# Between two layers of a transformer trunk: an overflow branch ahead of the last down projection, eight row fetches issued together, a store on another queue

## The chip, the cores and the metric

The kernel runs on one core of one Trainium2 chip. The metric is the device time of one execution in microseconds (us); the times shown are medians of several executions.

## The reference, cut to what matters

Two layers work on 256 latent tokens and 256 context tokens of width 1024, in float32. Each layer is an attention mixer and then a mixture of 16 experts, of which each token takes two. The second layer (layer 1) has no experts for the context.

```python
for layer in range(DEPTH):                                   # DEPTH = 2
    ...                                                      # norm, w_in, four attention groups, w_out
    x = x + m_lat[5] * moe_ffn(h2, router_w, router_b, w_gate[layer], w_up[layer], w_down[layer])
    if need_ctx:                                             # layer 0 alone
        ctx = ctx + m_ctx[5] * moe_ffn(hc2, ...)

# in moe_ffn, for a block of tokens of expert e
(jax.nn.silu(xe @ w_gate[e]) * (xe @ w_up[e])) @ w_down[e]
y = jnp.zeros_like(hf).at[buf_t].add(yb * buf_w[:, None])    # two rows per token
```

## The kernel before, in words

Weights come as transfers of 1 MB through a ring of slots, all from SyncE's queue (`stream`, `pump`, line 125). `next_w` takes the next one, `done_w` gives its slot back and issues the next load that a free slot allows.

The experts of layer 0 are the class `Moe`. Each expert has room for 96 tokens (CAP). Its tokens are gathered from DRAM, `first` multiplies with gate and up, `hidden` makes the SwiGLU product and transposes it into `hT` (ACT evacuates it, line 1061), and `second` is the down projection. `second` has a main part for 64 tokens (`py`, line 1075) and a rest for the other 32 (`py2`, line 1081); the weights come in two blocks, `hf` 0 and 1, and for each block the main part runs and then the rest. `store` multiplies both with the gates on VectorE (lines 1100 and 1104), and POOL scatters the rows into the DRAM buffer `yd` with one indirect DMA each (line 991). The matrix products are pinned in their program order; all else is placed on the engines' queues by a scheduler at build time, which knows the data's dependencies and a program order as priority.

Where an expert got more than 96 tokens, `overflow` computes the others in a loop inside a conditional block. Each engine reads the counter `mxi` into a register (line 1144) and jumps over the body by itself (line 1145). With the inputs here the body isn't run. Behind a jump not into the body, an engine adjusts the semaphores that the body would have moved: SyncE waits for its DMA lanes, POOL for the lanes of its scatters, and then runs INC_SWDGE_SEM. The call stands behind the last expert.

Then layer 1 begins with `make_hT`. For each tile of 128 tokens (0 and 1 latent, 2 and 3 context) `combine` fetches both rows of each token from `yd` into a buffer `yy` (two DMAs of 512 KB from SyncE's queue, three buffers), adds them to x with the routing weights (VectorE, line 1224) and, for tiles 0 and 1, stores x to DRAM from SyncE's queue (line 1226), for a reload much later. Then ACT squares the tile (line 406), POOL and VectorE make the norm (lines 299, 418), TensorE transposes two tiles at a time (line 429), and the projections of layer 1 begin (line 469; their weights are split in two halves at lines 456 and 458).

Of the kernel before, what the change touches and what calls it, by code (L numbers as in the profile page):

```python
# [11 lines left out]
F32 = mybir.dt.float32  # L12
# [8 lines left out]
D = 1024  # L21
L = 2
# [3 lines left out]
NE = 16  # L26
# [26 lines left out]
def body(tc, a, dbg=None):  # L53
    nc = tc.nc
    ctx = ExitStack()
    V, S, G, PE = nc.vector, nc.scalar, nc.gpsimd, nc.tensor

    def pool(name, bufs=1, space=None, stack=None, side=None):
        kw = {} if space is None else dict(space=space)
        if side is not None:  # L60
            kw["side"] = side
        return (stack or ctx).enter_context(tc.tile_pool(name=name, bufs=bufs, reuse_waits="tile", **kw))
# [9 lines left out]
    def psum(tag):  # L72
        return ps.tile([128, 512], F32, name=tag, bufs=dict(mm=2, ada=1, tr=2, S=2, o=1)[tag])
# [44 lines left out]
    def drop_ring(tag):  # L118
        assert all(x[0] != tag for x in used)
        slots_free[:] = [x for x in slots_free if x[0] != tag]  # L120


    def stream(out, in_):
        with tc.issue_after(state["dma"]) if state["dma"] is not None else nullcontext():
            state["dma"] = nc.sync.dma_start(out, in_).ins

    def pump():
        while slots_free and state["emit"] < len(jobs):
            nm, view, src = jobs[state["emit"]]
            xs = [y for y in slots_free if y[0] == "a" or nm[0] in "eo"]  # L130
            if not xs:
                break
            x = xs[0]
            slots_free.remove(x)
            t = slot(x)
            tv = t.rearrange("p (k n) -> p k n", n=view)
            stream(tv, src.rearrange("(k p) n -> p k n", p=128))
            issued.append((nm, x, tv))
            state["emit"] += 1

    def next_w(nm):
        if not issued:
            pump()
        n, tag, t = issued.pop(0)
        assert n == nm, (n, nm)
        used.append(tag)
        return t


    def done_w(n=1):  # L150
        for _ in range(n):
            slots_free.append(used.pop(0))
        pump()
# [66 lines left out]
    X = {}  # L220
# [559 lines left out]
    x1d = dram.tile([256, D], F32, name="x1d")  # L780

    class Moe:
# [281 lines left out]
        def second(self, e):  # L1064
            l, hT = self.l, self.hT
            py = psum("S")
            py2 = psum("S") if self.CAP > 64 else None
            for hf in range(2):
                wd = next_w(f"e{l}")
                for g in range(2):  # L1070
                    f = 2 * hf + g
                    for c in range(self.tiles_m):
                        m = 128 // self.tiles_m
                        t, h = c % (64 // m), 512 * (m * c // 64)
                        self.order(PE.matmul(py[m * c:m * c + m], lhsT=hT[:, f, m * t:m * t + m], rhs=wd[:, g, h:h + 512],  # L1075
                                             start=f == 0, stop=f == 3))
                if py2 is not None:
                    for g in range(2):
                        f = 2 * hf + g
                        for c in range(4):  # L1080
                            self.order(PE.matmul(py2[32 * c:32 * c + 32, 0:256],
                                                 lhsT=hT[:, 4 + f % 2, 32 * (f // 2):32 * (f // 2) + 32],
                                                 rhs=wd[:, g, 256 * c:256 * c + 256], start=f == 0, stop=f == 3))
                done_w()
            self.store(e, py, py2)


# [19 lines left out]
        def experts(self, p2):  # L1107
            self.p2, self.xt = p2, {}
            self.start()
            self.fetch(0)  # L1110
            p = self.first(0, lambda: self.fetch(1))
            for e in range(NE):
                q = self.next(e, p)
                self.second(e)
                p = q

# [72 lines left out]
        def general(self, ei, xT):  # L1189
            l, p2 = self.l, self.p2  # L1190
            pgs = []
            for nm in ("w_gate", "w_up"):
                pg = psum("mm")
                for k in range(8):
                    wk = p2.tile([128, 1, 512], F32, name="wk", bufs=2)
                    nc.sync.dma_start(wk, a[nm][l, bass.ds(ei, 1), 128 * k:128 * k + 128].rearrange("e p n -> p e n"))
                    PE.matmul(pg, lhsT=xT[:, k], rhs=wk[:, 0], start=k == 0, stop=k == 7)
                pgs.append(pg)
            sg, h = self.wide()
            S.activation(sg, pgs[0], AF.Silu)  # L1200
            V.tensor_mul(h, sg, pgs[1])
            pt = psum("tr").rearrange("p (q n) -> p q n", n=128)
            for k in range(4):
                PE.transpose(pt[:, k], h[:, 128 * k:128 * k + 128], ident)
            hT = p2.tile([128, 4, 128], F32, name="hT", bufs=2)
            S.activation(hT, pt, AF.Copy)
            y = p2.tile([128, D], F32, name="yo")
            for hf in range(2):
                py = psum("S")
                for f in range(4):  # L1210
                    wk = p2.tile([128, 1, 512], F32, name="wk", bufs=2)
                    nc.sync.dma_start(wk, a["w_down"][l, bass.ds(ei, 1), 128 * f:128 * f + 128,
                                                      512 * hf:512 * hf + 512].rearrange("e p n -> p e n"))
                    PE.matmul(py, lhsT=hT[:, f], rhs=wk[:, 0], start=f == 0, stop=f == 3)
                V.tensor_copy(y[:, 512 * hf:512 * hf + 512], py)
            return y


        def combine(self, t, scr):
            yy = scr.tile([128, 2, D], F32, name="yy", bufs=3)  # L1220
            for k in range(2):
                stream(yy[:, k], yd[self.l][256 * t + k:256 * t + 256:2])
            for k in range(2):
                V.scalar_tensor_tensor(X[t], yy[:, k], self.wts[:, t, k:k + 1], X[t], op0=OP.mult, op1=OP.add)
            if t < 2:
                nc.sync.dma_start(x1d[128 * t:128 * t + 128], X[t])


    class MoeOnChip(Moe):
# [232 lines left out]
    for l in range(L):  # L1462
# [8 lines left out]
        hT = [hp.tile([128, 8, 512], F32R, name=f"hT{i}") for i in range(2)]  # L1471
# [31 lines left out]
        g = GROUPS[-1]  # L1503
# [9 lines left out]
        scr = pool(f"op{l}", stack=stR, side=P)  # L1513
# [5 lines left out]
        moe = (Moe if l < L - 1 else MoeOnChip)(l, tiles, pers, scr)  # L1519
# [20 lines left out]
        p2 = pool(f"moe{l}", stack=stM, side=P)  # L1540
        if l < L - 1:

            moe.g5 = {}
            for s in range(len(tiles) // 2):
                g = moe.g5[s] = p2.tile([128, 768], F32, name=f"g5{s}")
# [11 lines left out]
                nc.scalar.dma_start(moe.gate[64 * c:64 * c + 64], amd[r:r + 1].to_broadcast([64, 512]))  # L1557
        with ExitStack() as stE:
            moe.experts(pool(f"moee{l}", stack=stE, side=P))
            if l < L - 1:  # L1560
                moe.overflow()
        drop_ring("c")
        drop_ring("b")
        stB.close()
# [117 lines left out]
```

## Time and profile before

| | us |
|---|---|
| median of three runs | 1228.17 |
| lowest and highest of them | 1224.29, 1228.35 |
| the profiled execution | 1229.28 |
| its span, first to last instruction | 1227.5 |
| TensorE busy in the span | 1119.5 (91%) |
| VectorE, ACT, POOL busy | 568.3, 417.2, 239.9 |

The span is what the trace covers; its zero is the first instruction. Busy counts instructions that an engine executes; jumps, semaphore waits and the issue of a DMA belong to the sequencer in front of the engine and stand under the engine's name with a q. "PEld" is TensorE's weight load, and PEldq the sequencer that serves both. In a timeline the bracket behind a line is the engine's idle time before it, and what ended it.

### The profile page before, as it was taken

The page shows a single profiled execution, that of the slowest core. Times are in us where ns is not written, and L with a number is a line of the kernel's source. Part 1 is how long each engine was busy: PE and PEld are TensorE (multiplying, and loading weights), DVE is VectorE, ACT ScalarE, POOL GpSimd, SP SyncE. Part 2 cuts the span into 40 slices and gives each one's busy share as a digit, 9 for nine tenths or more (in the row PEclk, how much of TensorE's full clock was granted, in tenths as well). Part 3 has the DMA queues.
Part 4 walks back from the last instruction along what each step waited for, and adds up shares of the span by engine and source line. Part 5 has one row for each costly group of instructions (what it writes and reads, how often), then busy time and mean ns, then how long its engine had stood idle before and what let it go on. Part 6 is the DMA issues. An engine that isn't in the chain of part 4 may idle for free. (4 is left out here: it accounts for less than half of the span.)

```text
span 1227.5 us, 21408 instructions
## 1 busy us (share of the span) xinstructions
PE 1119.5 (91%) x8495; PEld 654.6 (53%) x8495; DVE 568.3 (46%) x1545; ACT 417.2 (34%) x1003; POOL 239.9 (20%) x265
## 2 busy tenths in 40 slices
PE   4999999999999949999999992899999979999996
PEld 2677667676645424444444432888887443443432
DVE  4465766556433563232222225976775442332322
ACT  3445455446314312111111112665664221221211
POOL 1241220131111531212111113623231100000000
PEclk9999999999999969999999996998999989999998
DMA  9746445374570849999999966221325979999995
GB/s 304 258 168 241 177 168 194 123 274 143 201 274 17 326 125 340 373 380 386 373 370 367 390 235 226 78 70 36 129 70 176 350 268 393 393 393 394 394 394 229
DMA packets 134640, 313.00 MB, mean 255 GB/s; under 512 B 7212, under 2 KB 38448, under 8 KB 129408
## 3 DMA queue, kind: packets, MB, share of 16 engines
q1 hardware_dynamic: 127936, 294.19, 66.2%
q0 software_dynamic: 3840, 8.40, 2.1%
q10 hardware_dynamic: 2752, 8.91, 2.0%
q8 instruction: 71, 1.16, 0.4%
q14 instruction: 41, 0.34, 0.1%
HBM read 305.11 MB, written 10.55 MB: 257 GB/s over the span
## 5 line engine op out<-in xcount | busy, mean ns | idle before, releaser
L469 PE MATMUL mm<-ws,hT 128*128 128x256 f32 x1488 | 230.6, 297 | 3.7 <-DVE hT L508 1.8
L469 PEld LDWEIGHTS mm<-ws,hT 128*128 128x128 f32 x1488 | 201.3, 195 | 40.7 <-issue 26.2
L1022 PE MATMUL mm<-wb,xT 128*32 128x512 f32 x912 | 118.1, 604 | 0.0
L299 POOL TENSOR_TENSOR hss<-hss,mhalf 128x4 f32<-128x4 f32 (+2 forms) x56 | 67.2, 1203 | 183.8 <-DVE hss L298 171.3
L675 ACT ACTIVATE p<-S,nm 128x512 f32<-128x512 f32 (+1 forms) x120 | 73.7, 616 | 67.3 <-DVE nm L665 40.5
L665 DVE TENSOR_REDUCE nm<-S 128x1 f32<-128x512 f32 (+1 forms) x120 | 70.6, 597 | 27.0 <-PE S L640 22.9
L769 PE MATMUL mm<-wa,t4k 128*128 128x512 f32 x144 | 70.6, 611 | 0.0
L991 POOL DMA_INDIRECT yd<-y,idx x32 | 37.7, 1180 | 167.0 <-DVE y L1100 162.1
L1022 PE MATMUL mm<-wb,xTb 128*64 128x512 f32 x240 | 63.2, 596 | 0.9 <-DMA wb<-in_w_up_dram 0.9
L318 PE MATMUL ada<-wa,sc 128*32 128x512 f32 x320 | 62.6, 619 | 0.0
L1022 PEld LDWEIGHTS mm<-wb,xT 128*32 128x32 f32 x912 | 31.1, 111 | 52.5 <-issue 46.7
L1075 PE MATMUL S<-wb,hT 128*32 128x512 f32 (+1 forms) x360 | 56.0, 593 | 0.0
L648 PE MATMUL tr<-ident,p 128*128 128x128 f32 x320 | 51.4, 279 | 4.0 <-ACT p L675 3.7
L456 ACT ACTIVATE ws<-wa 128x512 fp32r<-128x512 f32 x80 | 48.8, 630 | 17.1 <-PE mm L469 7.4
L716 PE MATMUL o<-PT,v 128*64 128x256 f32 x320 | 54.5, 390 | 0.1
L615 PE MATMUL tr<-identr,sk 128*128 128x128 f32 x312 | 48.2, 257 | 6.5 <-DVE sk L612 4.5
L458 POOL TENSOR_TENSOR ws<-wa,ws 128x512 fp32r<-128x512 f32 x20 | 27.7, 1387 | 133.2 <-ACT ws L456 108.4
L1022 PE MATMUL mm<-wc,xTb 128*64 128x512 f32 x144 | 50.6, 596 | 0.0
L1061 ACT ACTIVATE hT<-tr 128x384 f32<-128x384 f32 (+1 forms) x32 | 14.0, 438 | 105.7 <-PE tr L1058 68.3
L648 PEld LDWEIGHTS tr<-ident,p 128*128 128x128 f32 x320 | 36.8, 141 | 21.8 <-ACT p L675 10.7
L458 DVE TENSOR_TENSOR ws<-wa,ws 128x512 fp32r<-128x512 f32 x60 | 43.5, 738 | 8.5 <-ACT ws L456 8.3
L615 PEld LDWEIGHTS tr<-identr,sk 128*128 128x128 f32 x312 | 35.6, 146 | 19.5 <-issue 10.3
(327 smaller groups left out, 1910.9 us busy)
## 6 DMA issues: line engine op xcount, KB each, us to landing
wb<-in_w_up_dram SPq DMA_DIRECT2D x49, 1024.0 KB
wa<-in_ada_w_dram SPq DMA_DIRECT2D x48, 1024.0 KB
wb<-in_w_gate_dram SPq DMA_DIRECT2D x38, 1024.0 KB
wb<-in_w_down_dram SPq DMA_DIRECT2D x30, 1024.0 KB
wa<-in_w_down_dram SPq DMA_DIRECT2D x22, 1024.0 KB
wa<-in_w_in_dram SPq DMA_DIRECT2D x20, 1024.0 KB
wc<-in_w_gate_dram SPq DMA_DIRECT2D x11, 1024.0 KB
wa<-in_w_gate_dram SPq DMA_DIRECT2D x10, 1024.0 KB
```

The lines of the kernel that those rows point to most:

```text
L299: state["pow"] = G.tensor_tensor(out, x, mhalf[:x.shape[0], :x.shape[1]], op=OP.pow).ins
L318: PE.matmul(pa[32 * c:32 * c + 32], lhsT=sc[:, k], rhs=w[:, 0, 512 * c:512 * c + 512], start=k == 0, stop=k == 7)
L458: (G if cnt["lo"] % 4 == 0 else V).tensor_sub(x[:, 1], r, x[:, 0].bitcast(F32))
L469: PE.matmul(acc, lhsT=lh[:, k, c], rhs=wp[k // 2][:, rh, k % 2], start=first and k == 0 and i == 0, stop=last and k == 7 and i == 2)
L615: PE.transpose(pt[:, i], sk[:, i], identr)
L648: PE.transpose(pt[:, i], p[:, k0 + 128 * i:k0 + 128 * i + 128], ident)
L665: V.tensor_reduce(nm[:, 0:1], s[:, k0:512], axis=AX.X, op=OP.min)
L675: S.activation(p[:, k0:512], s[:, k0:512], AF.Exp, bias=nm_, scale=scale, accum_out=z)
L716: PE.matmul(o[64 * c:64 * c + 64, 256 * j:256 * j + 256], lhsT=v[:, 2 * st + kc, vc:vc + 64], rhs=PTs[c][:, kc], start=kc == 0, stop=kc == ...
L769: PE.matmul(acc, lhsT=self.yT[key][:, t // 2, i, 128 * (t % 2):128 * (t % 2) + 128], rhs=w[key][:, i, 512 * h:512 * h + 512], start=n == 0 ...
L1022: self.order(PE.matmul(pa[m * c:m * c + m], lhsT=xT[:, 4 * hk + k, m * t:m * t + m], rhs=w[m * c // 64][:, k], start=hk == 0 and k == 0, s ...
L1075: self.order(PE.matmul(py[m * c:m * c + m], lhsT=hT[:, f, m * t:m * t + m], rhs=wd[:, g, h:h + 512], start=f == 0, stop=f == 3))
```

## The change

The call of `overflow` moves from behind the experts to between `hidden` and `second` of the last one, expert 15. In `second` of that expert, both blocks of the main part run first, then both of the rest, and both weight slots are given back at the end. The body of the branch gets a tile `hTg` of its own in place of a turn in the ring `hT`. `yy` has four buffers in place of three, and x is stored from ACT's queue.

```diff
-            for hf in range(2):
-                wd = next_w(f"e{l}")
+
+            def main(hf, wd):
                 for g in range(2):
...
-                if py2 is not None:
-                    for g in range(2):
-                        f = 2 * hf + g
-                        for c in range(4):
-                            self.order(PE.matmul(py2[32 * c:32 * c + 32, 0:256],
-                                                 lhsT=hT[:, 4 + f % 2, 32 * (f // 2):32 * (f // 2) + 32],
-                                                 rhs=wd[:, g, 256 * c:256 * c + 256], start=f == 0, stop=f == 3))
-                done_w()
+
+            def rest(hf, wd):
+                for g in range(2):
+                    f = 2 * hf + g
+                    for c in range(4):
+                        self.order(PE.matmul(py2[32 * c:32 * c + 32, 0:256],
+                                             lhsT=hT[:, 4 + f % 2, 32 * (f // 2):32 * (f // 2) + 32],
+                                             rhs=wd[:, g, 256 * c:256 * c + 256], start=f == 0, stop=f == 3))
+
+            if py2 is not None and e == NE - 1:
+
+                wd = [next_w(f"e{l}") for _ in range(2)]
+                for part in (main, rest):
+                    for hf in range(2):
+                        part(hf, wd[hf])
+                done_w(2)
+            else:
+                for hf in range(2):
+                    wd = next_w(f"e{l}")
+                    main(hf, wd)
+                    if py2 is not None:
+                        rest(hf, wd)
+                    done_w()
             self.store(e, py, py2)
@@ experts
                 q = self.next(e, p)
+                if e == NE - 1:
+                    self.overflow()
                 self.second(e)
@@ general
-            hT = p2.tile([128, 4, 128], F32, name="hT", bufs=2)
+            hT = p2.tile([128, 4, 128], F32, name="hTg")
@@ combine
-            yy = scr.tile([128, 2, D], F32, name="yy", bufs=3)
+            yy = scr.tile([128, 2, D], F32, name="yy", bufs=4)
...
             if t < 2:
-                nc.sync.dma_start(x1d[128 * t:128 * t + 128], X[t])
+                nc.scalar.dma_start(x1d[128 * t:128 * t + 128], X[t])
@@ body
             moe.experts(pool(f"moee{l}", stack=stE, side=P))
-            if l < L - 1:
-                moe.overflow()
```

## Rows read from the trace of the kernel before

**Rows 1.** Windows: stretch, us, busy us of PE PEld DVE ACT POOL, clock, DMA share, GB/s
```profile
740.00:760.00 20.00, 1.75 (x7) 1.38 (x8) 9.11 (x10) 2.44 (x5) 3.55 (x5) 0.50 0.72 243
```
**Rows 2.** Timeline of PE, last down projection: start us, us, engine, line, operation
```profile
729.71 1.92 PE L1075 MATMUL S<-wa,hT 128*32 128x512 f32 x16 [0.64 <-ACT hT L1061]
731.45 1.05 PE L1081 MATMUL S<-wa,hT 128*32 128x256 f32 x16
...
734.03 1.05 PE L1081 MATMUL S<-wb,hT 128*32 128x256 f32 x16
```
**Rows 3.** Timeline of DVE and POOL behind that product
```profile
734.28 0.69 DVE L1100 TENSOR_TENSOR y<-S,gsel 128x512 f32<-128x512 f32 x1 [5.24 <-PE S L1075]
...
735.14 0.42 DVE L1104 TENSOR_TENSOR y<-S,gsel 128x256 f32<-128x256 f32 x1 [0.17 <-PE S L1081]
735.25 0.97 POOL L991 DMA_INDIRECT yd<-y,idx  x1 [4.27 <-DVE y L1100]
736.53 1.09 POOL L991 DMA_INDIRECT yd<-y,idx  x1 [0.30 <-DVE ws L458]
```
**Rows 4.** Line 991, issue to landing: scatters of 728 to 732, then of 736.3 to 738
```profile
DMA to landing us min/median/max: 6.1/6.6/7.2
...
DMA to landing us min/median/max: 5.9/5.9/5.9
```
**Rows 5.** Lines 1145 and 1144, sequencers: ns min/median/max, first to last start us
```profile
L1145 PEldq COMPARE_BRANCH  x1: 8348/8348/8348, 733.8 to 733.8; - x1
...
L1145 DVEq COMPARE_BRANCH  x1: 72/72/72, 738.0 to 738.0; - x1
...
L1145 POOLq INC_SWDGE_SEM  x1: 1144/1144/1144, 742.5 to 742.5; - x1
...
L1144 PEldq TENSOR_LOAD <-mxi x1: 487/487/487, 733.2 to 733.2; - x1
```
**Rows 6.** Timeline of SP behind the branch
```profile
743.79 1.78 SPq L125 DMA_DIRECT2D yy<-yd  x4
750.43 0.32 SPq L1226 DMA_DIRECT2D x1d<-x  x1
...
755.54 1.43 SPq L125 DMA_DIRECT2D yy<-yd  x2
```
**Rows 7.** Timeline of DVE and PE: first and last adds to x, second transposes
```profile
747.80 2.61 DVE L1224 SCALAR_TENSOR_TENSOR x<-yy,wts,x 128x1024 f32<-128x1024 f32 x2 [9.74 <-DMA yy<-yd]
...
758.91 1.54 PE L429 MATMUL tr<-ident,xn 128*128 128x128 f32 x6 [4.21 <-DVE xn L418]
...
762.33 1.28 DVE L1224 SCALAR_TENSOR_TENSOR x<-yy,wts,x 128x1024 f32<-128x1024 f32 x1
...
763.66 2.17 DVE L1224 SCALAR_TENSOR_TENSOR x<-yy,wts,x 128x1024 f32<-128x1024 f32 x1
```
**Rows 8.** Line 1075, 726 to 736, TensorE's sequencer waits: columns as rows 5
```profile
L1075 PEldq EVENT_SEMAPHORE  x1: 1643/1643/1643, 726.8 to 726.8; - x1
```
**Rows 9.** Line 1408, the branch of layer 1, TensorE's sequencer: columns as rows 5
```profile
L1408 PEldq COMPARE_BRANCH  x1: 3422/3422/3422, 1218.6 to 1218.6; - x1
```
**Rows 10.** Waits of SP, 726 to 760: who, whom, us in total, times, longest
```profile
SPq L1145 <- SPq L1145: 7.0, 2, 5.2
```
**Rows 11.** Windows: first fetches, then the first projections of layer 1
```profile
745.00:750.00 5.00, 0.00 (x0) 0.00 (x0) 2.17 (x2) 0.00 (x0) 0.00 (x0) 0.50 0.93 337
...
764.00:769.00 5.00, 4.19 (x33) 3.82 (x32) 5.00 (x7) 3.21 (x6) 4.26 (x4) 1.00 0.10 36
769.00:780.00 11.00, 9.09 (x69) 8.05 (x69) 10.52 (x23) 7.44 (x18) 7.81 (x6) 1.00 0.16 53
```
**Rows 12.** Waits of PE, 758 to 800: columns as rows 10
```profile
PE tr L615 <- DVE sk L612: 2.2, 3, 0.9
PE ada L469 <- POOL ws L458: 1.5, 1, 1.5
```
**Rows 13.** Line 362, DMA issues on ACT's queue: columns as rows 5
```profile
L362 ACTq DMA_DIRECT2D sb<-amd x2: 326/410/495, 340.2 to 341.6; - x2
```

## The prediction

> **What bounds the kernel now.** I read the page first (where TensorE is idle), then TensorE's busy time by stretches, then the timeline of each engine around the layer boundary, then the sequencer rows of the branch. TensorE is the engine to watch: it is busy for 91% of the span, and its largest hole is the boundary between the layers, where it works 1.75 us out of 20 at a granted clock of 0.50 [rows 1]. So the question is what decides when the hole ends.
>
> The hole begins when the last down projection ends: it starts at 729.71, as soon as ACT's hT is there, and ends at 734.03 + 1.05 = 735.08 [rows 2]. VectorE makes y and y2 of it, and POOL issues one scatter for each, the second one at 736.53 [rows 3]. That one lands 5.9 us later, at 742.4 [rows 4]. Only then does POOL, which has passed the branch in the meantime, run the step that adjusts its DMA semaphores for the branch not taken: 1.14 us from 742.5 [rows 5]. At 743.79 SyncE issues the first four fetches, at 750.43 the store of x's tile 0, and only behind it the next two fetches; the last two go out at 755.54 [rows 6], behind the second store. TensorE has its second token tile at 758.91, 15.1 us after the first fetch [rows 7]. I call the first fetch's start T0; the sum is the shift of T0, plus what changes between T0 and the work behind 758.91.
>
> TensorE's own branch takes 8.35 us [rows 5], from 733.8 to 742.1. It costs nothing today: TensorE has no work then, and the scatter lands at 742.4 anyway.
>
> **Part 1: the branch ahead of the last down projection, TensorE.** TensorE's sequencer stands at that product's first matmul from 726.8 on, waiting 1.64 us [rows 8]. In the changed kernel it reads the counter there instead (0.49 us [rows 5], and 0.1 to the next), and is at the branch at 727.4. The product now stands behind the jump. Its length is not in the trace at this place. Lower end: 3.4 us, TensorE's jump at the end of the program [rows 9]; upper end: the 8.35 of today. SyncE's jump over the same body kept it from its next instruction for 5.2 us [rows 10]. Free isn't excluded, since VectorE's jump took 0.07 us [rows 5], but both of TensorE's were long. I take 5.2, since SyncE's jump is the nearest in time and over the same body, and lies between the two of TensorE. So the jump ends at 732.6, and the product starts 0.3 later (weight load and matmul) at 732.9 instead of 729.71: **+3.2 us**, bounds 0 to +6.4.
>
> [...]
>
> **Part 2: main blocks first.** The two blocks of the main part come first: one takes 1.74 us from start to the next part's start (729.71 to 731.45) [rows 2], so py is complete after 1.74 + 1.9 = 3.64 us, the rest after 5.37 as before. VectorE's y takes 0.69 and the first scatter follows 0.28 later [rows 3]: start + 4.7. The second needs y2 (5.37 + 0.06 + 0.42 + 0.1): start + 6.0, against 736.53 - 729.71 = 6.8 today: **-0.8 us**, because the second scatter no longer queues behind the first.
>
> **Part 3: the branch on POOL's queue.** POOL, too, has the last two scatters behind the branch now. Its adjusting step waits until the scatters issued so far have landed: today that is the second one of the last expert. In the changed kernel it is those of expert 14, the last issued at 730.0 and landing 6.1 us later (728.7 + 7.2 for the other) [rows 4], at 736.1; plus 0.1 and 1.14 makes 737.4. Then the first scatter cannot start before 737.6 and the second, 1.3 later (735.25 to 736.53), before 738.9. TensorE's side gives 732.9 + 6.0 = 738.9, so both say the same. What is saved, the 1.14 between landing and fetch, is paid here earlier.
>
> **T0**: 738.9 + 5.9 to land + 0.1 = 744.9 against 743.79: **+1.1 us**. With a free jump on TensorE it stays +1.1, by POOL's floor; without POOL's floor too, it is 729.71 + 6.0 + 6.0 = 741.7, **-2.1**; with 8.35 us it is 736.1 + 12.0 = 748.1, **+4.3**.
>
> **Part 4: eight fetches at once, four buffers.** The first four are issued at once today, and the DMA share is 0.93 from 745 on [rows 11], so tiles 0 and 1 don't come sooner. Tiles 2 and 3 do: SyncE holds their fetches back until x's stores have gone out at 750.43 and before 755.54 [rows 6]. The first fetch is added from 747.80, 4.0 us after T0, the last two from 762.33 and 763.66 [rows 7]. A fetch of 512 KB takes 1.6 us at the 337 GB/s of that stretch [rows 11], so the eighth would land some 4.0 + 7 x 1.6 = 15 us after T0, near 760. VectorE has no free time where today's last adds run: 5.00 of 5 us from 764 and 10.52 of 11 behind it [rows 11]. Moved ahead of that, they give VectorE 1.28 + 2.17 = 3.4 us [rows 7] back. TensorE's waits behind 759 that more room on VectorE and POOL could shorten are 1.5 and 2.2 us in sum [rows 12]. Bounds: 0, if TensorE's order is not limited by them, to -3.4. I take **-1.0**: TensorE is busy over 9 of 11 us there, so most of the room goes nowhere. There's also a loss possible: the order of VectorE's queue is fixed in advance, and an add of tile 2 placed ahead of tile 1's norm would hold the chain by its 1.28 us.
>
> **Part 5: x stored from ACT.** An issue on ACT's queue takes 0.33 to 0.50 us [rows 13]. Each stands where ACT is about to square the same tile. For tile 0 VectorE is later anyway; for tile 1 it lies on the chain: **+0.4**, at most +0.9. SyncE loses 0.64 us of issue and the two waits, priced in part 4. The load of the next weights behind them comes earlier; nobody waits for that one.
>
> **Part 6: hTg** is a buffer of its own in the branch's body, which doesn't run: 0. The third weight load of the next layer now follows the whole product (done_w(2)): issued near 738, landed before 745, ahead of the fetches: 0.
>
> **Sum**: +1.1 - 1.0 + 0.4 = +0.5 us, on a profiled execution of 1229.28 us (span 1227.5); the median of the three runs is 1228.17, 0.1% lower. Added to the median: 1228.7 us. The terms are differences of a few us, so they carry over. Behind the boundary a shift should reach the end, since TensorE, then the weight stream, follow without a large hole.
>
> **Rivals.**
> *It gains.* TensorE's jump is short and POOL's adjusting step does not hold the scatters: T0 falls by 2.1; VectorE's 3.4 us come through whole: -2.1 - 3.4 + 0.4 = -5.1, 1223 us; if tile 1's chain also gets shorter by one VectorE add, below 1222. For: VectorE's jump was short, and VectorE is the fullest engine from 764 on. Against: both of TensorE's jumps, and scatters that land 6 us after issue.
> *It loses.* TensorE's jump takes the 8.35 us that it took before, now with the product behind it: the product starts at 736.1, after 7 us of idleness on TensorE. The clock was granted at 0.50 in the hole that followed 735.08 [rows 1]; if the same happens inside this pause, the product of 5.37 us takes up to twice that. T0: +4.3 + about 2.7 (half of it at half clock) = +7.0; with +0.4 and nothing returned, 1228.2 + 7.4 = 1235.6. Point from which it decides: the jump over 5.2 us; every us beyond is one us of T0. For: the same jump of the same engine. Against: the same jump at the end took 3.4 [rows 9].
> *The fetches aren't really at once.* SyncE is held in the middle by a buffer still read by a scatter, or the DMA engines are full anyway, and tile 3's earlier arrival finds VectorE's order unchanged: nothing returned, +1.1 + 0.4 = +1.5: 1229.7.
>
> **How the numbers follow.** Forecast (T0 1 to 2 later, about 1 returned), 1227 to 1231: 0.47. It gains: 0.23, of which 0.11 beyond 0.5% (6.1 us, about what a measurement of this kernel can tell from no change; below 1222.0). It loses: 0.18, of which 0.13 beyond 1234.3. Not at once: 0.12. So faster 0.11, same 0.76, slower 0.13. The range runs from 1221 to 1235.5, just under the whole gain's 1222 and up to the whole loss, which leaves out the outer parts of these two tails, under 0.2 together.
>
> **What would show it.** Right: TensorE's jump lies near 727.4 and is longer than 3 us, and the last down projection starts after 731; POOL's adjusting step lies between expert 14's and expert 15's scatters, ending near 737; the eight fetches go out within 4 us from about 745; the last add to x comes before 762. Wrong: a jump under 0.2 us, a first scatter of the last expert before 736, or a first fetch before 743 (then the gain), a first fetch after 747 or clock 0.50 inside the product (then the loss). A new order of layer 1's work, which the trace of before can't show, would make the whole prediction wrong.

## The result, and the profile after

| | before | after |
|---|---|---|
| median | 1226.64 us (1220.79 to 1232.27) | 1237.11 us (1233.28 to 1242.83) |
| ratio | 1 | **1.0093**, 95% interval 1.0072 to 1.0114 |
| profiled execution / span | 1229.28 / 1227.5 us | 1236.72 / 1234.9 us |

The change makes the kernel 0.9% slower, by some 10.5 us. The forecast was 1228.7 with a range up to 1235.5: wrong in its number and in its range.

Places are counted below from H, the end of ACT's last `hT` of layer 0, which the last down projection needs. ACT's timeline, first before, then after:

```profile
729.16 0.49 ACT L1061 ACTIVATE hT<-tr 128x384 f32<-128x384 f32 x1 [5.33 <-PE tr L1058]
```

```profile
726.46 0.49 ACT L1061 ACTIVATE hT<-tr 128x384 f32<-128x384 f32 x1 [5.33 <-PE tr L1058]
```

So H is 729.16 + 0.49 = 729.65 before and 726.46 + 0.49 = 726.95 after. From H to the end it is 497.85 us before and 507.99 after: +10.1. Single executions scatter: a second profile of the kernel before (e5 below) has its first fetch 1.45 us sooner behind H and its end 2.7 us sooner than the one that the prediction rests on. So a difference under 3 us in the places is not read from two profiles alone.

**TensorE.** The timeline around the last down projection, after: start us, us, engine, line, operation, and in brackets the idle time before and what ended it (answers [rows 2]).

```profile
726.08 0.28 PE L1058 MATMUL tr<-ident,hh 64*128 64x64 f32 x2
732.62 3.64 PE L1075 MATMUL S<-wa,hT 128*32 128x512 f32 x16 [6.26 <-DVEq L1162]
736.01 3.01 PE L1075 MATMUL S<-wb,hT 128*32 128x512 f32 x16
738.83 1.05 PE L1082 MATMUL S<-wa,hT 128*32 128x256 f32 x16
739.69 1.05 PE L1082 MATMUL S<-wb,hT 128*32 128x256 f32 x16
```

Two things are new. The product starts at 732.62, 5.67 behind H instead of 0.06, and what released it is not TensorE's own jump but **VectorE's sequencer at the branch** (DVEq L1162). And the first block takes 3.64 us, where the one of before took 1.92 [rows 2].

The line of the branch, after (columns and counterpart as [rows 5]):

```profile
L1162 PEldq COMPARE_BRANCH  x1: 5452/5452/5452, 724.7 to 724.7; - x1
...
L1162 DVEq COMPARE_BRANCH  x1: 72/72/72, 726.5 to 726.5; - x1
...
L1162 PEldq EVENT_SEMAPHORE  x1: 51/51/51, 730.3 to 730.3; - x1
L1162 DVEq EVENT_SEMAPHORE  x1: 21/21/21, 732.5 to 732.5; - x1
L1162 POOLq INC_SWDGE_SEM  x1: 1095/1095/1095, 733.4 to 733.4; - x1
...
  PE S L1075: 6.3, 1
```

TensorE's jump lasts 5.45 us and its sequencer is past the branch at 730.3. VectorE's record of the branch is 0.07 us as before, but its next instruction, the semaphore step behind the branch, comes at 732.5: 6.0 us after the branch. Before, the branch stood at 738.0 [rows 5] and that step 0.6 us behind it:

```profile
L1145 DVEq EVENT_SEMAPHORE  x1: 21/21/21, 738.6 to 738.6; - x1
```

The length of VectorE's jump is thus not in the duration of its record, but in the gap to the next instruction. It is no wait for another engine: the semaphore that this step waits for is moved, up to then, by VectorE's own instructions alone, and the last of those had ended at 726.34.

What the engines stand still for is suggested by the DMA queues, and borne out by e3 below. From 722 to 736 the kernel after has these loads of instructions (queue, kind: packets, MB, share of the DMA engines):

```profile
q8 instruction: 2, 0.03, 0.9%
q14 instruction: 5, 0.04, 0.7%
```

Six of the seven start between 724.7 and 732.5.

The stretch of the product (columns as [rows 1]), first after, then before:

```profile
732.60:740.80 8.20, 8.12 (x64) 2.64 (x64) 0.69 (x1) 0.00 (x0) 0.75 (x1) 0.66 0.00 1
```

```profile
729.70:735.10 5.40, 5.37 (x64) 1.98 (x64) 0.69 (x1) 0.63 (x1) 0.98 (x1) 1.00 1.05 341
```

The same 64 matmuls take 8.12 us at a granted clock of 0.66 in the mean instead of 5.37 at 1.00. The granted clock is at 0.50, the lower of the two levels that its records have, for 6.8 us from 4.4 behind H (731.4 to 738.2): it fell while TensorE stood idle at the branch and came back inside the product.

**POOL**, after: start us, us, operation (answers [rows 3]).

```profile
740.05 0.97 POOL L991 DMA_INDIRECT yd<-y,idx  x1 [11.78 <-DVE y L1115]
741.03 0.27 POOL L386 TENSOR_TENSOR ropes<-tab 128x32 f32<-128x32 f32 x1
...
743.39 1.28 POOL L389 TENSOR_TENSOR ropes<-tab 128x16 f32<-128x16 f32 x2
744.83 1.26 POOL L991 DMA_INDIRECT yd<-y,idx  x1 [0.16 <-issue]
```

```profile
DMA to landing us min/median/max: 2.6/5.9/6.9
```

Between the last two scatters now stand the rope tables of layer 1, from 741.03 to 744.67, 3.64 us. Before, they began at 737.61, behind both scatters:

```profile
737.61 0.55 POOL L386 TENSOR_TENSOR ropes<-tab 128x32 f32<-128x32 f32 x1
```

VectorE's `y2` of the kernel after was ready at 741.79, and the second scatter goes out at 744.83:

```profile
741.37 0.42 DVE L1119 TENSOR_TENSOR y<-S,gsel 128x256 f32<-128x256 f32 x1 [1.60 <-PE S L1082]
```

The line of landings above is that of the four scatters from 726 on: the last one takes 2.6 us, the one before it 6.0.

**SyncE** issues all eight fetches in one go, with the whole wait for the second scatter behind it (answers [rows 6]):

```profile
747.53 5.57 SPq L125 DMA_DIRECT2D yy<-yd  x8
```

**VectorE, ACT and TensorE up to tile 1's transposes**, after (answers [rows 7]). The lines are three answers, one for each engine:

```profile
758.29 2.60 DVE L1241 SCALAR_TENSOR_TENSOR x<-yy,wts,x 128x1024 f32<-128x1024 f32 x2
760.80 0.15 DVE L298 TENSOR_SCALAR ss<-ss 128x1 f32<-128x1 f32 x1
761.14 1.28 DVE L1241 SCALAR_TENSOR_TENSOR x<-yy,wts,x 128x1024 f32<-128x1024 f32 x1 [0.19 <-DMA yy<-yd]
762.34 0.75 DVE L418 TENSOR_SCALAR xn<-x,ss 128x1024 f32<-128x1024 f32 x1
...
758.36 0.19 ACT L406 ACTIVATION_READ_ACCUMULATOR z<-x 128x1 f32 x1
...
763.14 1.54 PE L429 MATMUL tr<-ident,xn 128*128 128x128 f32 x6 [3.96 <-DVE ss L298]
```

ACT has tile 1's sum of squares at 758.55, but VectorE takes it up at 760.80, behind two additions to x of tile 2, and makes tile 1's `xn` at 762.34, behind one of tile 3. From the first fetch to tile 1's transposes it is 15.6 us, against 15.1 before and 14.8 in the second profile of before.

The ledger of the two profiles, in us behind H:

| | before | after | change |
|---|---|---|---|
| product starts | 0.06 | 5.67 | +5.6 |
| product ends | 5.43 | 13.79 | +8.4 |
| last scatter issued | 6.88 | 17.88 | +11.0 |
| first fetch, T0 | 14.14 | 20.58 | +6.4 |
| tile 1's transposes | 29.26 | 36.19 | +6.9 |
| last product of the projections | 205.52 | 216.61 | +11.1 |
| end | 497.85 | 507.99 | +10.1 |

### The profile page after: what moved, and what is told of

Same layout as the page of the kernel before. It is cut to its first block, busy times and chain, and to the rows that moved or that the text cites. A ratio compares the mean times of both kernels' runs of the same rounds, so it can differ in the third digit from the quotient of the medians.

```text
span 1234.9 us, 21408 instructions
## 1 busy us (share of the span) xinstructions
PE 1123.3 (91%) x8495; PEld 655.5 (53%) x8495; DVE 567.6 (46%) x1545; ACT 417.2 (34%) x1003; POOL 236.0 (19%) x265
## 5 line engine op out<-in xcount | busy, mean ns | idle before, releaser
L665 DVE TENSOR_REDUCE nm<-S 128x1 f32<-128x512 f32 (+1 forms) x120 | 70.5, 596 | 24.6 <-PE S L640 20.5
L1075 PE MATMUL S<-wa,hT 128*32 128x512 f32 (+1 forms) x312 | 43.3, 616 | 6.5 <-DVEq L1162 6.3
```

Of the source, the lines that this page charges most:

```text
L665: V.tensor_reduce(nm[:, 0:1], s[:, k0:512], axis=AX.X, op=OP.min)
```

## Experiments

Theory A was from the start that the branch is what costs (TensorE and the product stand still behind it), its rival that the fetches and the store do. Ratios are to the kernel before, with 95% intervals.

### One half of the change at a time: e1, e2

e1 has the branch ahead, main blocks first and `hTg`, and keeps three buffers `yy` and SyncE's store. e2 is the kernel before with these two lines:

```diff
-            yy = scr.tile([128, 2, D], F32, name="yy", bufs=3)
+            yy = scr.tile([128, 2, D], F32, name="yy", bufs=4)
-                nc.sync.dma_start(x1d[128 * t:128 * t + 128], X[t])
+                nc.scalar.dma_start(x1d[128 * t:128 * t + 128], X[t])
```

> The branch ahead of the last down projection and its main blocks first, alone: three buffers yy, x stored from SyncE as before. Theory A (the loss is the code loading of TensorE's and VectorE's jumps in front of the product, and the product at half clock): the product starts some 5.6 us later after hT than before, the first fetch some 6 us later, and the time is 6 to 10 us above before (ratio 1.005 to 1.008). Theory B (the loss comes from the fetches: adds of tiles 2 and 3 in VectorE's queue ahead of tile 1's norm, ACT's store): the time is within 3 us of before, and the late product costs nothing because something else ends later.

> Four buffers yy and x stored from ACT, alone; the branch stays behind the experts. Theory A: the first fetch is where it was before (14.1 us after hT), the last add ends some 3 us earlier, and the time is 0 to 3 us below before. Theory B: tile 1's transposes come 17 to 18 us after the first fetch instead of 15.1, because the adds of tiles 2 and 3 stand in front of tile 1's norm, and the time is 3 to 10 us above before.

e1: **1.0098** (1.0073 to 1.0124), more than theory A's 1.005 to 1.008. The branch alone costs as much as the whole change, and the trace repeats it: the product starts 5.69 behind H, takes 7.89 us, and T0 is 20.37.

```profile
736.44 3.64 PE L1075 MATMUL S<-wa,hT 128*32 128x512 f32 x16 [6.28 <-DVEq L1162]
...
736.40:744.40 8.00, 7.89 (x64) 2.62 (x64) 0.70 (x2) 0.01 (x1) 0.76 (x1) 0.68 0.00 1
```

e2: **1.0046** (1.0027 to 1.0066). The half that the prediction counted as a gain of 0.6 us is a loss of its own. The additions of tiles 2 and 3 stand in front of tile 1's norm, as in the kernel after, and T0 to the transposes takes 15.8 us (theory B: 17 to 18). But T0 itself is only 11.42 behind H in this profile, so the transposes come 27.23 behind H, no later than in the two profiles of before (29.26 and 27.49). Where the lost time of e2 arises behind them is not shown.

### Which part of the second half: e8, e7

e8 is before with the store alone on ACT's queue. e7 is e2 with the additions of tiles 2 and 3 issued behind tile 1's `xn`:

```diff
-                V.tensor_scalar(xn, X[t], r, None, op0=OP.mult)
+                state["xn"] = V.tensor_scalar(xn, X[t], r, None, op0=OP.mult).ins
...
+            if s == 0:
+                state["xn1"] = state["xn"]
...
-            for k in range(2):
-                V.scalar_tensor_tensor(X[t], yy[:, k], self.wts[:, t, k:k + 1], X[t], op0=OP.mult, op1=OP.add)
+            with tc.issue_after(state["xn1"]) if t > 1 else nullcontext():
+                for k in range(2):
+                    V.scalar_tensor_tensor(X[t], yy[:, k], self.wts[:, t, k:k + 1], X[t], op0=OP.mult, op1=OP.add)
```

> Only the store of x moves to ACT's queue; three buffers yy. Theory B1 (early adds of tiles 2 and 3 cost): with SyncE free of the stores, tile 2's fetches go out with the first four, the adds move up in part, and the time is 1 to 4 us above before. Theory B2 (the store on ACT costs, 0.4 to 0.9 us): 0 to 1 us above before. If neither, 0 to 2 us below.

> The fetch part alone (as e2_fetch_alone), and the adds of tiles 2 and 3 queued on VectorE behind tile 1's norm. Theory B (early adds cost the fetch part its gain): tile 1's transposes come 13 us after the first fetch instead of 15.8, and the time is 3 to 6 us below e2_fetch_alone (ratio to before 0.998 to 1.002). If the adds' place doesn't matter, the ratio stays at 1.004 to 1.005, and the loss of the fetch part lies in layer 1's order or in ACT's store.

e8: **1.0034** (1.0010 to 1.0057). With three buffers the eight fetches still go out one behind the other, over 7.55 us:

```profile
739.94 7.55 SPq L125 DMA_DIRECT2D yy<-yd  x8
```

So it was the two stores in SyncE's queue that held the fetches back; with them gone the additions move up in VectorE's order, and T0 to the transposes takes 16.1 us. What the fourth buffer adds lies within the intervals of e8 and e2.

e7: **0.9997** (0.9977 to 1.0017). With tile 1's norm first, the loss of e2 is gone; the two intervals don't overlap. So the order of the additions is what costs. VectorE's timeline of e7, tile 1's `xn` and what follows it:

```profile
749.99 0.75 DVE L418 TENSOR_SCALAR xn<-x,ss 128x1024 f32<-128x1024 f32 x1 [0.67 <-POOL ss L299]
750.66 1.28 DVE L1227 SCALAR_TENSOR_TENSOR x<-yy,wts,x 128x1024 f32<-128x1024 f32 x1
```

T0 to the transposes takes 13.1 us, 1.7 to 2.0 less than in the two profiles of before, and yet the time is that of before. Why the gain at the boundary doesn't show in the time is not explained by these runs. The step itself is steady over the profiles: T0 to the transposes takes 15.6 to 16.1 us in the six kernels with the additions early, 14.6 to 15.1 in the five profiles with the store on SyncE's queue, and 12.6 to 13.1 in the three kernels with the additions in order (e7, e11, e12).

### The length of the jump: e3, e9

The loop in the body of the branch runs once instead of four times, which makes the code that is jumped over a quarter as long. In e3 this is done to the kernel after, in e9 to the kernel before, where the product is ahead of the branch.

```diff
-                    for b in range(-(-(128 * nt - CAP) // 128)):
+                    for b in range(1):
```

> The changed kernel with the branch's body cut to a quarter (one block of 128 overflowing tokens per expert instead of four; the body isn't run with these inputs). It leaves out the treatment of tokens beyond 224 of one expert. Theory A: both jumps are short (under 1 us each), so the product starts within 1 us of hT and runs at full clock; the first fetch then comes 1 to 2 us later than before by POOL's wait for expert 14's scatters, and the time is within 3 us of before. If the lost time is not in the jumps (theory B), the time stays 8 to 11 us above before. In between (+3 to +6): a jump of 3.4 us remains on one of the two engines.

> The kernel before with the branch's body cut to a quarter, the branch still behind the experts. It leaves out the treatment of tokens beyond 224 of one expert, which don't occur here. Theory A says that a jump behind the experts costs nothing, since TensorE has no work then: time within 2 us of before, though TensorE's jump is under 1 us instead of 8.35. A time 3 us or more below before would mean that the long jump did cost something there (by SyncE's waits, or by code blocks in the DMA engines' way of the scatters).

e3: **1.0020** (1.0002 to 1.0038), 0.7% below the kernel after. The branch and the first matmuls of the product in e3:

```profile
L1162 PEldq COMPARE_BRANCH  x1: 353/353/353, 727.3 to 727.3; - x1
...
L1162 DVEq COMPARE_BRANCH  x1: 72/72/72, 729.1 to 729.1; - x1
...
L1162 DVEq EVENT_SEMAPHORE  x1: 21/21/21, 729.6 to 729.6; - x1
...
729.76 1.93 PE L1075 MATMUL S<-wa,hT 128*32 128x512 f32 x16 [0.85 <-DVEq L1162]
```

With a quarter of the body TensorE's jump takes 0.35 us and VectorE's gap 0.5; the product starts 0.25 behind H and takes 5.37 us at a granted clock of 1.00. No load of instructions starts between 727.3 and 729.7, where the kernel after had six while its engines stood at the branch. So the length of what is jumped over carries the loss, through the late start and through the clock, and not the branch as such. What is left over, 0.2%, may be the additions' loss, which e3 still has (T0 to the transposes 15.7 us); no run took it out of e3.

The short body changes one thing more. POOL's adjusting step runs at 730.1 in e3, 0.2 us behind the issue of expert 14's second scatter, and the first scatter of expert 15 goes out 4.93 behind H: with one block in the body, the step doesn't wait for those scatters to land, as it does in the kernel after.

e9: **0.9991** (0.9973 to 1.0009). Behind the experts the length of the jump costs nothing that the times show: TensorE's was 2.45 us there, with no effect on the time beyond 0.3%.

### TensorE's wait for VectorE: e4

The product after the branch and the body's own product share the bank of PSUM called S, and VectorE empties it in both. e4 is the kernel after with the body's product in another bank, so that the last product need not wait for VectorE's part of the branch.

```diff
-                py = psum("S")
+                py = psum("mm")
```

> The changed kernel, with the body's own down projection in the PSUM banks mm instead of S, so that the last down projection doesn't wait for VectorE's side of the branch. Theory A: the product starts right behind TensorE's own jump (5 to 6 us long), some 3.2 us after hT instead of 5.7; the clock may stay up, and the time is 2 to 5 us below the changed kernel. If VectorE's jump doesn't matter, the time equals the changed kernel's (1.009 of before).

e4: **1.0097** (1.0069 to 1.0125). It doesn't tell the two apart as meant, because the order of the instructions, which is worked out anew for each kernel, changed too: with the bank free, 18 of the product's matmuls went ahead of the branch.

```profile
729.34 1.02 PE L1075 MATMUL S<-wb,hT 128*32 128x512 f32 x2
734.34 1.63 PE L1075 MATMUL S<-wb,hT 128*32 128x512 f32 x11 [3.98 <-PEq L1162]
```

It does show that TensorE need not wait for VectorE once the bank is not shared: those 18 ran from 727.60 on, while VectorE stood at the branch from 727.1 to 734.1. The rest came behind TensorE's own jump, 6.48 us in this place, which ended at 734.2 (PEq in the bracket). Cut in two by it, the product cost as much as in the kernel after: the first scatter went out 10.28 behind H, T0 was 17.77. The granted clock fell to 0.50 here too, for 3.4 us from 735.6 on, inside the second part of the product and behind a pause of 3.98 us. How much of the 5.6 us the bank alone would save was not measured.

### The kernel before once more: e5

> The kernel before, unchanged: a second profile of it. In its first profile the last two scatters took some 7 and 5.9 us to land, in the changed kernels' 2.3 to 4.3 us where no weight load was due beside them. If that first profile is typical, the first fetch starts again 14.1 us after the last hT (within 0.5). If it was a late one, it starts 11 to 12.5 us after it, and the true loss at the boundary is 2 to 3 us larger than the two profiles say.

The branch and the first fetches in this second profile:

```profile
L1145 PEldq COMPARE_BRANCH  x1: 5488/5488/5488, 730.4 to 730.4; - x1
...
738.93 1.77 SPq L125 DMA_DIRECT2D yy<-yd  x4
```

TensorE's jump at the old place is 5.49 us here and was 8.35 in the first profile [rows 5]; in e2, e7 and e8, which have the branch there too, it is 5.53 to 5.81, so the 8.35 is the odd one. The last scatter landed in 4.5 us instead of 5.9, and T0 is 12.69 behind H instead of 14.14, between the two cases expected. The rows that the prediction took as fixed durations vary by 3 and 1.4 us from one execution to the next.

### Mending the parts: e10, e11

e10 keeps the branch ahead with all four blocks, but as a loop at run time with one copy of the body, and issues the rope tables behind the last scatter; fetches and store are as before. e11 is e10 with four buffers, the store on ACT and the additions in order (e7).

```diff
-                    for b in range(-(-(128 * nt - CAP) // 128)):
+                    bcol = p2.tile([128, 1], F32, name="bcol")
+                    V.memset(bcol, -float(CAP))
+                    with tc.For_i(0, -(-(128 * nt - CAP) // 128), 1):
...
-                        V.tensor_scalar(posb, pos, -float(CAP + 128 * b), None, op0=OP.add)
+                        V.tensor_scalar(posb, pos, bcol, None, op0=OP.add)
+                        V.tensor_scalar(bcol, bcol, -128.0, None, op0=OP.add)
...
-        tables(l, GROUPS[0])
+        with tc.issue_after(state["sc"]) if l else nullcontext():
+            tables(l, GROUPS[0])
```

> The branch ahead of the last down projection with a short body (the blocks of 128 overflowing tokens as an inner loop at run time instead of four copies), layer 1's rope tables queued on POOL behind the last scatter, fetches and x's store as before. Theory A: both jumps are under 1 us, the product starts within 0.5 us of hT at full clock, the second scatter goes out 6 to 6.5 us after hT and lands by 9; the first fetch starts 8.5 to 10.5 us after hT against 12.7 and 14.1, and the time is 2 to 4 us below before (ratio 0.997 to 0.999). If something else than the jumps makes a branch ahead dear, it is 5 us or more above before.

> As e10_loop_body, with the eight fetches at once, x stored from ACT, and the adds of tiles 2 and 3 queued behind tile 1's norm: all that the change meant to do, without the three losses found. Theories A and B: the first fetch starts 8.5 to 10.5 us after hT, tile 1's transposes come 13 us later, and the time is 3 to 7 us below before (ratio 0.994 to 0.998). If the two parts' gains don't add, 0.997 to 1.000.

e10: **1.0007** (0.9985 to 1.0029), not the gain expected (0.997 to 0.999). The jump is 0.36 us, as in e3, with the whole work kept. The scatters go out at 4.93 and 6.97 behind H, but T0 is 12.15, where 8.5 to 10.5 was expected:

```profile
734.66 0.97 POOL L991 DMA_INDIRECT yd<-y,idx  x1 [3.59 <-DVE y L1115]
736.70 1.17 POOL L991 DMA_INDIRECT yd<-y,idx  x1 [1.07 <-DVE y L1119]
...
741.88 1.77 SPq L125 DMA_DIRECT2D yy<-yd  x4
```

The first fetch, which waits for the second scatter's landing, goes out 5.2 us after that scatter's issue. The windows of e10 show what moves in the meantime:

```profile
736.00:738.00 2.00, 0.00 (x0) 0.00 (x0) 2.00 (x4) 2.00 (x4) 1.28 (x2) 1.00 0.52 153
738.00:740.00 2.00, 0.00 (x0) 0.00 (x0) 0.95 (x2) 0.19 (x1) 2.00 (x8) 1.00 1.04 366
740.00:741.80 1.80, 0.00 (x0) 0.00 (x0) 0.00 (x0) 0.00 (x0) 1.80 (x6) 0.68 0.51 168
```

That is the third weight load of layer 1, which in this order is issued at 736.37, when the whole product has given both slots back. In e3 the second scatter goes out at 739.81, behind most of that load, and lands in 2.3 us. That the load holds the scatter back fits both, but no run moved the load alone: it stays a reading.

e11: **0.9976** (0.9956 to 0.9996), the lowest ratio of all, 1223.57 us: just clear of the kernel before, and 1.1% below the kernel after. T0 is 12.09 behind H, again later than the 8.5 to 10.5 expected. Its transposes of tile 1 come 12.6 us after T0, 24.68 behind H against 29.26 and 27.49 in the two profiles of before:

```profile
753.45 1.54 PE L431 MATMUL tr<-ident,xn 128*128 128x128 f32 x6 [0.91 <-DVE xn L418]
```

### The whole change, one mend at a time: e12, e13

e12 is the kernel after with the additions in order, e13 the kernel after with the tables behind the last scatter (both edits as above).

> The whole change, with the additions to x of tiles 2 and 3 issued behind the norm of tile 1, as in e7_adds_in_order. Theory A (the two losses add: the branch costs what e1 showed, and in the whole change too the additions stand in tile 1's chain): from the first fetch to tile 1's transposes 12.6 to 13.4 us in place of 15.6, and the time falls by some 0.4 to 0.5% from the whole change, to 1.004 to 1.006 of the kernel before. Rival B (behind the late product the additions no longer stand in the way, or what they free is eaten by the next wait, which would be why e1 and e2 don't add up to the whole change): 1.008 or more of the kernel before, whatever the stretch up to the transposes takes.

> The whole change, with the rope tables of the next layer issued on POOL behind the last scatter instead of between the last two (3.64 us of POOL). The product still starts 5.6 us late. Theory A (the second scatter, held by the tables, sets the first fetch together with the first one): the second scatter starts 14.3 to 14.6 us after the last hT in place of 17.9, the first fetch at 19.1 (the landing of the first scatter) to 20.2 in place of 20.6, and the time falls by 0.3 to 1.4 us: 1.0080 to 1.0092. Rival B (two scatters close together land no sooner than one behind the other, as in e10_loop_body, or the tables are missed by the rotation of layer 1): first fetch at 20.4 or later, and 1.0090 to 1.0110.

e12: **1.0061** (1.0033 to 1.0090). T0 to the transposes falls from 15.6 to 13.0 us, as theory A had it. The ratio falls by 0.3%, less than the 0.4 to 0.5% expected; its interval overlaps that of the kernel after and includes the rival's 1.008, so the times leave it open. VectorE's timeline of e12 has tile 1's `xn` 12.2 us behind the first fetch at 747.83, where the kernel after had 14.8:

```profile
760.01 0.75 DVE L418 TENSOR_SCALAR xn<-x,ss 128x1024 f32<-128x1024 f32 x1 [0.67 <-POOL ss L299]
```

e13: **1.0078** (1.0055 to 1.0102), expected 1.0080 to 1.0092. The second scatter goes out 14.99 behind H (expected 14.3 to 14.6) instead of 17.88, and T0 is 19.38 instead of 20.58: it is then the first scatter's landing, at 19.07, that sets it together with the second's.

```profile
748.34 1.17 POOL L991 DMA_INDIRECT yd<-y,idx  x1 [1.05 <-DVE y L1119]
...
752.73 5.72 SPq L125 DMA_DIRECT2D yy<-yd  x8
```

That the tables held the scatter is shown, by 2.9 us. The 1.2 us of T0 are less than the 1.45 by which two profiles of one kernel differ, and the two ratios, 1.0093 and 1.0078, have overlapping intervals: what the tables cost in the end is not shown.

## Why the prediction was wrong, point by point

**TensorE's jump (part 1).** Its place and length were right: at the branch 2.21 us ahead of H (727.44 in the time of before; said: 727.4), 5.45 us long (said: 5.2). That the length fits is in part luck: 5.2 was SyncE's jump, which took 4.6 us in the kernel after, and the only jump of TensorE's over this body that had been seen took 8.35. By the runs its length goes with the code that is jumped over: the same branch takes 0.35 us over a quarter of the body (e3, with no load of instructions meanwhile) and 0.36 over one copy in a loop (e10), and 5.33 to 5.61 over four copies (after, e1, e12, e13), which hold 160 matrix products and transposes in the kernel's text.

**The step that failed** is "the product starts 0.3 later", that is, that TensorE's own jump is all the product waits for. It waits for VectorE too, since the body uses the same bank of PSUM and VectorE frees it there (e4); and VectorE's jump, priced nowhere, took 6.0 us at the new place, until 732.5. That part of the prediction rested on the record "VectorE's jump took 0.07 us" [rows 5], which is the branch instruction alone; the gap to the next instruction, 0.6 us, stood in the same view and was not read. Term: +5.6 instead of +3.2. Why the same jump over the same body takes VectorE 0.6 us behind the experts and 6.0 here is open. One rival is the traffic of the weight loads: the DMA share was 0.88 from 726.5 to 732.5 after, and 0.34 from 738.0 to 738.6 before. No run changed the traffic alone.

**The clock.** The prediction had the half clock inside the product, but only for the second rival, from a jump of 8.35 us on. Here it came behind a pause of 6.26 us: the product took 8.12 us instead of 5.37, **+2.75** (the rival's estimate was 2.7). The prediction let that rival decide from a jump of 5.2 us on, at one us of T0 for each us beyond; the clock's part stood outside that slope.

**Main blocks first (part 2)** should have gained 0.8 because the second scatter no longer queues behind the first. It queued behind the rope tables instead: 3.64 us of POOL that the prediction had not counted as standing there. In the rows of before the second scatter follows the first at once [rows 3]; the tables stood behind both. e13 puts the loss at 2.9 us of issue; in T0 its one profile has 1.2 us less.

**POOL's adjusting step (part 3)** came where it was predicted: it ends at 734.50, 737.2 in the time of before (said: 737.4). The mechanism is right too: the steps of its wait at 733.0 and 733.1 follow the landings of expert 14's scatters, 732.93 and 733.12. It did not bind, because the product was later still; in e3 and e10 the floor isn't there at all, as said above.

**T0.** Said +1.1, measured +6.4. The 5.3 between them are 2.4 from VectorE's jump, 2.75 from the clock, 2.9 from the tables, 0.6 because VectorE's `y2` began 0.63 behind the end of the product instead of 0.06, less 3.3 because the last scatter landed in 2.6 us instead of the 5.9 that was assumed: 5.35. The last of these hid part of the others, and nobody had foreseen it.

**Fetches and store (parts 4 and 5).** The eight fetches go out one behind the other, 5.3 us from the first to the last (said: 4), and VectorE has the last addition 17.5 us after T0 against 22.0 before. But the gain of 1.0 was a loss: the case that part 4 named and gave no price in the sum, an addition of tile 2 ahead of tile 1's norm, is what VectorE's order came to, with three additions of 1.28 us instead of one. e2 and e7 put the price at 0.5% (1.0046 against 0.9997); e12's 0.3% inside the whole change is not clear of noise. By the traces it is 2.6 to 2.7 us at the transposes (e12 against after, e7 against e2), and the early additions are about one us worse there than the order of before; why the times show 4 to 6 us is open.

**What is left.** Up to tile 1's transposes the kernel after is 6.9 us behind (8.7 against the second profile of before). From there to the last product of the projections it takes 180.4 us, before 176.3. But e13, which keeps the additions and fetches of the kernel after, takes 175.7, and e12 181.6. The stretch follows the clock: once the granted clock has risen behind the boundary, it is at 0.50 again for 3.4 us of the stretch in e13, 6.83 before, 13.65 after and 20.5 in e12. The 64 matmuls of the last down projection went with the clock, 5.37 us at 1.00 and 8.12 at 0.66 in the mean, so a us at 0.50 is taken to cost half a us at most, and the 6.8 us between before and after make up to 3.4 of the 4.1 (an estimate from these rows). Whether the change brings this or one execution of many isn't shown, so the 4.1 us are not put down to the change. e1 leaves as much open: its profile ends 502.39 behind H, 4.5 to 7.3 us later than the two of before, where the medians differ by 11.9.

The halves don't add up either: e1's 0.98% and e2's 0.46% stand against 0.93% for the whole. The gap of 0.51 is more than the half-widths of the three intervals (0.26, 0.20 and 0.21) combined as independent errors, 0.39, and less than their plain sum. Where the rest of the sum goes is not settled.

**The rivals.** "It loses" was nearest, with 1235.6 and a chance of 0.18. Its mechanism, a long jump followed by a product at half clock, is what happened, with VectorE instead of TensorE as the last to arrive. Its sum left out the loss that part 4 named: with 2.7 us for it, it would have come to 1228.2 + 7.4 + 2.7 = 1238.3, on the other side of the time.

## What to carry to other kernels

A branch that is never entered was not free where work depended on it (e1: 1.0098): every engine that the next product needs, through its operands or through a buffer shared with the body, jumps on its own. On the path the price went with the amount of code jumped over (TensorE 5.45 us against 0.35, VectorE 6.0 against 0.5); behind the experts the same code cost VectorE 0.6. Before such a branch is put on the path, make its body short (one copy in a run-time loop: e10) and read the gap behind each engine's branch, not the branch's own duration. When transfers come earlier, the fixed order of a queue can let their consumers in ahead of more urgent work (e2: 1.0046), so pin the low-priority instructions behind the chain (e7: 0.9997), and look for what else moves into a gap that the change opens (the tables on POOL, 3.64 us).

## What the runs showed of the chip that was not expected

- The same jump over the same body varies with place and execution: TensorE 8.35 and 5.49 us behind the experts in two executions of one kernel, 5.33 to 5.61 ahead of the product in four kernels, 6.48 in the middle of it. VectorE's gap was 0.6 us behind the experts, 5.9 to 6.1 ahead of the product in the four kernels, and 6.9 in e4. With one block of body TensorE's was 2.45 us at the old place and 0.35 at the new one.
- An indirect scatter of one tile landed 2.3 to 7.5 us after its issue. The last ones of e3 and of the kernel after took 2.3 and 2.6 us at a DMA share of 0.41 and 0.17 meanwhile, the one before it in the kernel after 6.0 at 0.68, one of expert 14 in e7 7.5 at 1.06. But the last one of e5 took 4.5 at 0.39, so the share alone doesn't tell the time.
- A pause of TensorE of 6.26 us ahead of the product was followed by 6.8 us at a granted clock of 0.50, 5.6 of them inside the product; with a pause of 0.85 us (e3) the product ran at a granted clock of 1.00.
